# One plain feature block less in three feed-forward openings, and two norm broadcasts moved, in a two-layer encoder kernel

## The chip, the cores and the metric

The kernel runs on one core of one Trainium2 chip. The metric is the device time of one execution in microseconds (us), the median of several. TensorE (PE) does the matmuls, VectorE (DVE), ScalarE (ACT) and GpSimd (POOL) the elementwise work, and SyncE (SP) issues most of the loads of weights from memory.

## What is computed

A bidirectional encoder of two layers, 512 tokens (SEQ) of width 1024 (D_MODEL), all in float32. Each layer has a feed-forward half step, a block of mixers, a second feed-forward half step, and a gated embedding; a norm ends the whole.

```python
def rmsnorm(x, g):
    y = xf * lax.rsqrt(jnp.mean(xf * xf, axis=-1, keepdims=True) + EPS)
    return (y * g.astype(jnp.float32)).astype(x.dtype)
def swiglu(x, w_gate, w_up, w_down):
    return (jax.nn.silu(x @ w_gate) * (x @ w_up)) @ w_down
...
    for i in range(DEPTH):
        h = h + 0.5 * swiglu(rmsnorm(h, ffn1_norm[i]), ffn1_w_gate[i], ffn1_w_up[i], ffn1_w_down[i])
        ...
        h = h + y @ w_out[i]
        h = h + 0.5 * swiglu(rmsnorm(h, ffn2_norm[i]), ffn2_w_gate[i], ffn2_w_up[i], ffn2_w_down[i])
        e = rmsnorm(p[i] @ ple_w_proj[i], ple_post_norm[i])
        gate = jax.nn.sigmoid(rmsnorm(h, ple_gate_norm[i]) @ ple_w_gate[i])
        h = h + gate * e
    return rmsnorm(h, final_norm)
```

The hidden width of the feed-forward is 2816: 22 feature blocks of 128 (NF).

## The kernel before, in words

Activations lie with the features on the 128 partitions and the tokens along the free axis. Every float32 operand is split into a high part (rounded for the matmul, `hi`, names ending in h) and a low part (the rest, `lo`, names ending in l), and a product is three matmuls: high by high, high by low, low by high (`mm3`, L146). ACT makes the high parts (casts), DVE the low parts (L132, `lo_of`).

**Norm.** The sum of squares of a token comes out of a small matmul (`tok`, L195), DVE makes the inverse root (`rtok`, L163), and `bc` (L212) transposes it over all partitions into a bank of PSUM, which ACT copies to `rbc` (L214). The norm is applied after the matmul, since it scales whole tokens.

**A feed-forward** (`ffn`, called four times: ffn1 and ffn2 of layer 0, ffn1 and ffn2 of layer 1) goes through 22 feature blocks. The first `np0` are plain: a block has a gate chunk and an up chunk of weights (`Chunk`: load into `wraw`, cast to `whi` L347, low part `wlo` L132), and each chunk is 24 matmuls of 128x512 (`plain`, L147 to L149). `np0` is PLAIN0 in the first call and PLAIN in the others. A finished plain block is gated (`gated`, L373): DVE multiplies the gate's bank by the norm (L376), ACT takes Silu (L377, with a table load ahead of the first), DVE multiplies by the up bank (L379), ACT makes the high part `ah` (L381) and DVE the low part `al`. `gate(f)` starts this for block f, each `step()` takes every started block one stage on.

The other blocks are made with the Strassen-Winograd scheme: seven products p1 to p7 of half the size in each direction, 12 matmuls of 128x256 each (L597), in place of eight. They need sums of quarters of the weights (`qd` and `qa`, cast and split to `pw`: `parts`, L561 and L132; the sums S2 and S4 by DVE, `sums`, L582 and L584) and sums T1 to T4 of quarters of the input (`quarters` on ACT and POOL, `combined` L397 and L398 on DVE, then high parts `th` L402 and low parts `tl` L132). These input sums are made once per feed-forward, beside the plain blocks: the opening.

The order on TensorE at the first Strassen block u is p1(u), p5(u), p2(u), p6(u), p1(u+1), p7(u), p5(u+1), p4(u), p2(u+1), p3(u), and so on. p5 multiplies T1 with the weights S1. p6 adds into the bank of p1 after ACT copied it to `g1` (L624), and p7 adds into the same bank after ACT copied p6's sum to `g2` (L663). p7's own copy is `c22` (L673).

**What sets the order.** In `ffn` every engine runs its instructions in the order in which the code writes them. Stages are put into a list of items with planned times; loads and weight preparation (`tasks`) are put between the items by their lead times, so ACT and DVE run one fixed row of casts, gating and sums. The openings are `slabs` and `opening(n)` for the first call, `opening2` and `later(n)` for the others (n counts the chunks): in each, the matmuls of chunk n come first, then the next chunks' casts (`beside`), the input sums, `step()` and `gate`.

**The embedding's gate** (`ple`, L1391) for the last layer works on two halves of the tokens, b = 0 and 1, with eight output blocks m each: 24 matmuls of 128x256 per half block. Two norms are needed in its first half: that of h (`st.norm`) and that of the embedding e (`nm`). Banks of PSUM are eight, four each of the kinds `ps` and `pm`; `norm_banks` takes two `pm` banks. `post` multiplies the eight blocks of e by their norm (L1425, DVE), then `gate(i)` finishes a half block (L1417). Here only TensorE follows the written order.

Of the kernel before, what the change touches and what calls it, by code (L numbers as in the profile page):

```python
# [30 lines left out]
HALF = T // 2  # L31
LEAD = 5
H = T // 2
PLAIN = 3
PLAIN0 = 4
GROUPS = (5, 4, 4, 4, 5)
NA = max(GROUPS) + 1
QD = 6
# [28 lines left out]
CH = {}  # L67
# [28 lines left out]
def trunk(ctx: ExitStack, tc, xT, pT, pos, W, gains, cst, dftc, out):  # L96
# [195 lines left out]
            b = slice((base + k) * P, (base + k + 1) * P)  # L292
            mm3(o, hi[:, b], lo[:, b], st.hi[k], st.lo[k], k == 0, k == NK - 1)

    def ffn(l, cgu, cd, st, nxt, first=False):

# [3 lines left out]
        with tc.tile_pool(name="ap", bufs=1) as ap, tc.manual_schedule():  # L302
# [57 lines left out]
                    return [(lead + 6.0, self.load), (lead, prep)]  # L360


            np0 = PLAIN0 if first else PLAIN
            Th, Tl = [], []
            xgs, ts, side = {}, {}, []

            def step():

                for x in list(side):
                    if next(x, None) is None:  # L370
                        side.remove(x)
# [13 lines left out]
            def quarters(i):  # L385
                xg = xgs[i] = tile("pw", 6, [2, T])
                for j in range(2):
                    S.activation(xg[:, j], h[:, i + 4 * j], AF.Copy, scale=st.g(i + 4 * j))
                t = ts[i] = tile("pw", 6, [4, H])
                b11, b12, b22 = xg[:, 0, 0:H], xg[:, 0, H:T], xg[:, 1, H:T]  # L390
                G.tensor_tensor(t[:, 0], b11, b12, op=ALU.subtract)
                G.tensor_tensor(t[:, 1], b22, b12, op=ALU.subtract)

            def combined(i):

                xg, t = xgs.pop(i), ts[i]
                V.scalar_tensor_tensor(t[:, 2], t[:, 0], -1.0, xg[:, 1, H:T], op0=ALU.mult, op1=ALU.subtract)  # L397
                V.scalar_tensor_tensor(t[:, 3], t[:, 2], -1.0, xg[:, 1, 0:H], op0=ALU.mult, op1=ALU.subtract)  # L398

            def combined_high(i):  # L400
                Th.append(tile("th", 4, [4, H], F32R))
                S.copy(Th[i], ts[i])  # L402
# [5 lines left out]
            def gate(f):  # L408
                side.append(gated(f))
                next(side[-1])  # L410

            pairs = []
            chunks = [Chunk(cgu + n) for n in range(2 * np0)]
# [72 lines left out]
            def opening(n):  # L486
                def run():
                    plain(n)
                    beside(n)
                    if n == 4:  # L490
                        combined(3)
                    if n < 6:
                        combined_high(n - 2)
                    step()
                    for f in {5: (0, 1), 6: (2,), 7: (3,)}.get(n, ()):
                        gate(f)
                    if n < 6:
                        combined_low(n - 2)
                    if n == 4:
                        bc()  # L500

                return run

            def opening2():

                for ks in (range(NK - 1), range(NK - 1, NK)):
                    plain(0, ks)
                    plain(1, ks)
                chunks[2].high()
                chunks[2].low()  # L510
                quarters(0)
                quarters(1)
                for i in range(2):
                    combined(i)
                    combined_high(i)
                for i in range(2):
                    combined_low(i)
                tok()
                chunks[3].high()

            def later(n):
                def run():
                    plain(n)
                    beside(n)
                    if n == 2:
                        quarters(2)
                        quarters(3)
                    if n in (2, 3):
                        combined(n)
                        combined_high(n)  # L530
                    step()
                    if n > 2:
                        gate(n - 3)
                    if n in (2, 3):
                        combined_low(n)
                    if n == 2:
                        bc()

                return run
# [75 lines left out]
            def p1(u):  # L615
                U[u] = {"gate": Chunk(cgu + 2 * u)}

                def run():
                    d = U[u]
                    d["B"] = bank("ps")[:, 0:H]  # L620
                    hi, lo = d["gate"].hi, d["gate"].lo
                    product(u, "B", hi[:, 0:T], lo[:, 0:T], "B11", True)
                    d["g1"] = small("g1")
                    S.copy(d["g1"], d["B"])  # L624
                    step()

                return run, U[u]["gate"].tasks(2, 10.1)

            def p5(u):
                def run():  # L630
                    d = U[u]
                    d["E"] = bank("ps")[:, 0:H]
                    p = d["w", "S1"]
                    product(u, "E", p[:, 0], p[:, 1], "T1", True)
                    step()

                def prep():
                    parts(u, "S1")
                    sums(u)

                return run, load(u, "S1", 0, "A22") + [(7.0, prep)]

            def p2(u, after=None):
                def run():
                    d = U[u]
                    d["A"] = bank("pm")[:, 0:H]
                    hi, lo = d["gate"].hi, d["gate"].lo
                    product(u, "A", hi[:, T:2 * T], lo[:, T:2 * T], "B21", True)
                    V.tensor_tensor(d["g1"], d["g1"], d["A"], op=ALU.add)  # L649
                    G.tensor_tensor(d["g1"], d["g1"], st.rb[:, h1], op=ALU.mult)  # L650
                    step()
                    if after is not None:
                        finish2(after)

                return run, []
# [735 lines left out]
    def ple(l, st, nxt):  # L1391


        with tc.tile_pool(name="pp", bufs=2) as pp, tc.manual_schedule(engines={mybir.EngineType.PE}):
# [82 lines left out]
            for b in range(2):  # L1477
                pgs = []
                acc = pp.tile([P, T // 2], F32, tag="acc", name="acc")
                accs.append(acc)  # L1480
                for m in range(NK):
                    if b == 0:
                        raw = pp.tile([P, CHUNK], F32, tag="gr", name="gr", bufs=3)
                        nc.sync.dma_start(raw, W[l, CH["gate"] + m])
                        gw.append((pp.tile([P, CHUNK], F32R, tag="gh", name="gh", bufs=NK),
                                   pp.tile([P, CHUNK], F32R, tag="gl", name="gl", bufs=NK)))
                        split(*gw[m], raw)
                    pgs.append(bank("pm" if m % 2 else "ps")[:, 0:T // 2])
                    for k in range(NK):
                        kb = slice(k * P, (k + 1) * P)  # L1490
                        mm3(pgs[m], gw[m][0][:, kb], gw[m][1][:, kb], st.hi[k][:, half[b]], st.lo[k][:, half[b]],
                            k == 0, k == NK - 1)
                    if b == 0 and m in (0, 2):
                        norm_banks.append(bank("pm"))
                    if b == 0 and m == 0:
                        st.rt = st.norm.tok(pt=norm_banks[0])
                    if b == 0 and m == 2:
                        st.rb = st.norm.bc(st.rt, pb=norm_banks[0])
                        r = nm.tok(pt=norm_banks[1])
                    if b == 0 and m == 3:  # L1500
                        post(r, norm_banks[1])
                    if b == 1 and m == 2:
                        final_tok(0)
                    if b == 1 and m == 4:
                        final_out(0)
                    for i in ((), (), (), (0, 1, 2, 3), (m,))[min(m, 4)] if b == 0 else (m,):
                        gate(i, pgs[i], half[b])
                        sq = acc if i == 0 else pp.tile([P, T // 2], F32, tag="sq", name="sq")
                        S.activation(sq, h[:, i, half[b]], AF.Square)
                        if i < NK - 1:  # L1510
                            S.activation(h[:, i, half[b]], h[:, i, half[b]], AF.Copy, scale=fg(i))
                        if i >= NK - 2:
                            sqs[b].append(sq)
                        elif i:
                            V.tensor_tensor(acc, acc, sq, op=ALU.add)
# [11 lines left out]
    st = stage(0, "ffn1")  # L1527
    for l in range(L):
        s_mix, s_f2, s_pl = stage(l, "mix"), stage(l, "ffn2"), stage(l, "pleg")
        ffn(l, CH["f1gu"], CH["f1d"], st, s_mix, l == 0)  # L1530
        mix(l, s_mix, s_f2)
        ffn(l, CH["f2gu"], CH["f2d"], s_f2, s_pl)
        st = stage(l + 1, "ffn1") if l + 1 < L else None
        ple(l, s_pl, st and st.chunk)
# [135 lines left out]
```

## Time and profile before

| | |
|---|---|
| median of 3 runs | 2003.66 us (2003.05 to 2003.98) |
| the profiled execution | 2003.73 us |
| its span on the core | 2002.0 us |
| mean granted clock of TensorE | 0.996 |
| busy: PE, DVE, ACT, POOL | 1974.2, 1552.8, 1012.5, 412.5 us |
| chain that ended last | PE 92%, DVE 4%, ACT 2% |

The profiled execution lies within the runs; 1.73 us of it are around the span. Times in the views below count from the start of the span. A row of a timeline has the start, the length, the engine, the line, the operation, what it writes and reads, and in brackets the idle time before it with what ended it. An instruction's length overlaps with the next one's start.

### The profile page before, as it was taken

How to read it: one execution, taken by the hardware profiler on the slowest of the kernel's cores; microseconds unless marked ns; L12 is line 12 of the kernel's file. 1: busy time of each engine (PE TensorE's matmuls, PEld its weight loads, DVE VectorE, ACT ScalarE, POOL GpSimd, SP SyncE). 2: the span in 40 equal slices, each digit the busy share in tenths (PEclk: the TensorE clock that was granted, in tenths of full speed). 3: DMA queues.
4: the chain of work that ended last, by engine and by line, in shares of the span. 5: the costliest groups of instructions: out<-in, count | busy, mean ns of one | idle time of the engine just before them, and what ended most of it. 6: DMA issues, size and time to landing. Idle time of an engine off the chain costs nothing.

```text
span 2002.0 us, 32174 instructions
## 1 busy us (share of the span) xinstructions
PE 1974.2 (99%) x12370; PEld 1763.1 (88%) x12370; DVE 1552.8 (78%) x2599; ACT 1012.5 (51%) x1945; POOL 412.5 (21%) x470
## 2 busy tenths in 40 slices
PE   9999999999999999999999999999999999999997
PEld 7999999888789899998888999988977899999987
DVE  7788777677768778877886888776796677778876
ACT  6454445456645344546563444454665554445463
POOL 2132224001002223331021332320000122223400
PEclk9999999999999999999999999999999999999999
DMA  5456653321125555552255556622221266655431
GB/s 188 134 154 158 169 138 103 104 89 42 52 85 153 161 151 149 145 155 95 97 148 142 154 146 152 163 82 93 81 66 47 98 157 158 168 139 153 122 126 43
DMA packets 99707, 248.20 MB, mean 124 GB/s; under 512 B 11184, under 2 KB 14128, under 8 KB 99552
## 3 DMA queue, kind: packets, MB, share of 16 engines
q1 hardware_dynamic: 75216, 203.08, 30.8%
q0 software_dynamic: 21664, 39.56, 12.2%
q10 hardware_dynamic: 2672, 3.49, 0.6%
q8 instruction: 97, 1.59, 0.3%
q14 instruction: 58, 0.48, 0.1%
HBM read 242.42 MB, written 2.10 MB: 122 GB/s over the span
## 4 chain that ended last, share of the span: by engine, by line
PE 92%; DVE 4%; ACT 2%; DMA 1%; issue 1%; ACTq 0%; DVEq 0%; POOL 0%; POOLq 0%; SPq 0%
PE ps L597 32%; PE ps L147 9%; PE ps L148 9%; PE ps L149 9%; PE pm L149 8%; PE pm L147 8%; PE pm L148 8%; PE pm L597 5%; PE ps L827 1%; PE ps L828 1%; PE ps L829 1%; PE ps L1280 1%; DVE wlo L132 1%; DMA wraw<-in_W 1%; PE pm L195 0%
## 5 line engine op out<-in xcount | busy, mean ns | idle before, releaser
L597 PE MATMUL ps<-th,pw 128*128 128x256 f32 x2400 | 457.2, 283 | 1.1 <-ACT c L673 1.1
L132 DVE TENSOR_TENSOR wlo<-wraw,whi 128x1024 fp32r<-128x1024 f32 (+4 forms) x273 | 348.2, 1276 | 53.1 <-ACT whi L347 32.3
L597 PEld LDWEIGHTS ps<-th,pw 128*128 128x128 f32 x2400 | 384.9, 192 | 2.3 <-ACT c L673 1.3
L597 PE MATMUL ps<-tl,pw 128*128 128x256 f32 x1200 | 339.6, 283 | 0.0
L347 ACT CAST whi<-wraw 128x512 fp32r<-128x512 f32 (+1 forms) x260 | 200.5, 802 | 225.6 <-PE pm L148 114.9
L597 PEld LDWEIGHTS ps<-tl,pw 128*128 128x128 f32 x1200 | 229.8, 192 | 1.1
L132 DVE TENSOR_TENSOR pw<-qd,pw 128x512 fp32r<-128x512 f32 x225 | 181.2, 805 | 15.0 <-ACT pw L561 9.7
L573 POOL DMA_DIRECT2D qd<-in_W x150 | 130.9, 927 | 252.0 <-DMA qd<-in_W 242.4
L147 PE MATMUL pm<-ah,whi 128*128 128x512 f32 x392 | 154.7, 395 | 0.0
L149 PE MATMUL pm<-ah,wlo 128*128 128x512 f32 x392 | 154.6, 394 | 0.0
L148 PE MATMUL pm<-al,whi 128*128 128x512 f32 x392 | 154.3, 394 | 0.0
L663 ACT COPY g<-ps 128x256 f32<-128x256 f32 x75 | 27.9, 372 | 224.8 <-PE ps L597 223.4
L135 ACT CAST ah<-g 128x256 fp32r<-128x256 f32 x150 | 59.1, 404 | 151.7 <-DVE g L689 138.9
L561 ACT CAST pw<-qd 128x512 fp32r<-128x512 f32 x225 | 129.6, 616 | 0.0
L135 ACT CAST whi<-wraw 128x1024 fp32r<-128x1024 f32 (+4 forms) x80 | 77.4, 969 | 98.5 <-PE ps L148 48.3
L132 DVE TENSOR_TENSOR pw<-qa,pw 128x512 fp32r<-128x512 f32 x150 | 117.3, 782 | 12.2 <-ACT pw L561 12.2
L147 PE MATMUL ps<-ah,whi 128*128 128x512 f32 x312 | 123.0, 394 | 0.0
L149 PE MATMUL ps<-ah,wlo 128*128 128x512 f32 x312 | 122.9, 394 | 0.0
L148 PE MATMUL ps<-al,whi 128*128 128x512 f32 x312 | 122.8, 394 | 0.0
L597 PE MATMUL ps<-xh,pw 128*128 128x256 f32 x600 | 119.9, 283 | 0.0
L650 POOL TENSOR_TENSOR g<-g,rbc 128x256 f32<-128x256 f32 x75 | 65.8, 878 | 219.3 <-DVE g L649 219.3
L608 POOL TENSOR_TENSOR g<-g,c 128x256 f32<-128x256 f32 x75 | 66.3, 884 | 208.5 <-ACT g L607 208.5
(382 smaller groups left out, 5241.5 us busy)
## 6 DMA issues: line engine op xcount, KB each, us to landing
wraw<-in_W SPq DMA_DIRECT2D x239, 512.0 KB, 3.4
qd<-in_W SPq DMA_DIRECT2D x225, 256.0 KB, 4.2
qd<-in_W POOLq DMA_DIRECT2D x150, 256.0 KB, 4.7
gr<-in_W SPq DMA_DIRECT2D x8, 512.0 KB, 3.7
wraw<-in_W SPq DMA_DIRECT2D x8, 320.0 KB, 3.1
wraw<-in_dftc SPq DMA_DIRECT2D x4, 516.0 KB, 3.3
wraw<-in_W SPq DMA_DIRECT2D x8, 256.0 KB, 3.8
wraw<-in_W SPq DMA_DIRECT2D x4, 408.0 KB, 3.0
```

Source lines behind the costliest of these rows:

```text
L132: V.tensor_tensor(lo, x, hi.bitcast(F32), op=ALU.subtract)
L135: S.copy(hi, x)
L147: mm(o, wh, xh, start=first, stop=False)
L148: mm(o, wh, xl, start=False, stop=False)
L149: mm(o, wl, xh, start=False, stop=last)
L347: S.copy(self.hi[:, b], self.raw[:, b])
L561: S.copy(p[:, 0], U[u][src])
L573: nc.gpsimd.dma_start(U[u][name], up[:, T:2 * T] if add == "A22" else gate[:, 0:T], accum_op=ALU.add)
L597: mm(U[u][o], x[:, b], y, start=first and i + j == 0, stop=i == 3 and j == 2, skip_group_check=not first)
L608: G.tensor_tensor(d["g2"], d["g2"], d["c22"], op=ALU.mult)
L650: G.tensor_tensor(d["g1"], d["g1"], st.rb[:, h1], op=ALU.mult)
L663: S.copy(d["g2"], d["B"])
```

## The change

PLAIN goes from 3 to 2 and PLAIN0 from 4 to 3 (three of the four feed-forwards have one plain block less and one Strassen block more); the third call, ffn1 of layer 1 (`late`), keeps three, and there the norm's broadcast and the input sums are spread over one chunk more. The gated blocks' stages are put by a table, `plan`, of which the places S1, S2 and S3 are behind p1, p5 and p2 of the first Strassen block; `None` is a `step()`, a number a `gate`. In `ple` of the last layer the broadcast of h's norm and the sums of e's norm come behind half block 3 and not 2, `post` and the first gates behind half block 5 and not 3, and the first half's final norm two half blocks later in the second half. Lines behind L412 move by 7 to 10: the product's matmul is L604, the casts L568, the copies of `g1`, `g2` and `c` L631, L673 and L683, the sums L589 and L591.

```diff
-PLAIN = 3
-PLAIN0 = 4
+PLAIN = 2
+PLAIN0 = 3
...
-    def ffn(l, cgu, cd, st, nxt, first=False):
+    def ffn(l, cgu, cd, st, nxt, first=False, late=False):
...
-            np0 = PLAIN0 if first else PLAIN
+            np0 = PLAIN0 if first or late else PLAIN
...
+            S1, S2, S3 = 100, 101, 102
+            plan = ({5: (0, 1), S1: (None, None, 2), S2: (None,), S3: (None,)} if first else
+                    {4: (0, 1), 5: (None, None, 2), S1: (None,), S2: (None,)} if late else
+                    {3: (None, 0), S1: (None, 1), S2: (None,), S3: (None,)})
+
+            def gating(n):
+
+                for f in plan.get(n, ()):
+                    step() if f is None else gate(f)
...
                     if n < 6:
                         combined_high(n - 2)
-                    step()
-                    for f in {5: (0, 1), 6: (2,), 7: (3,)}.get(n, ()):
-                        gate(f)
+                    gating(n)
...
-                for i in range(2):
+                for i in range(2 - late):
                     combined(i)
                     combined_high(i)
...
                     if n == 2:
                         quarters(2)
+                    if n == 2 + late:
                         quarters(3)
-                    if n in (2, 3):
-                        combined(n)
-                        combined_high(n)
-                    step()
-                    if n > 2:
-                        gate(n - 3)
-                    if n in (2, 3):
-                        combined_low(n)
-                    if n == 2:
+                    if n - late in (1, 2, 3)[not late:]:
+                        combined(n - late)
+                        combined_high(n - late)
+                    gating(n)
+                    if n - late in (1, 2, 3)[not late:]:
+                        combined_low(n - late)
+                    if n == 2 + late:
                         bc()
...
                     S.copy(d["g1"], d["B"])
-                    step()
+                    if u == np0:
+                        gating(S1)
...
-                    if b == 0 and m in (0, 2):
+                    if b == 0 and m in (0, 3):
                         norm_banks.append(bank("pm"))
...
-                    if b == 0 and m == 2:
+                    if b == 0 and m == 3:
                         st.rb = st.norm.bc(st.rt, pb=norm_banks[0])
                         r = nm.tok(pt=norm_banks[1])
-                    if b == 0 and m == 3:
+                    if b == 0 and m == 5:
                         post(r, norm_banks[1])
-                    if b == 1 and m == 2:
+                    if b == 1 and m == 4:
                         final_tok(0)
-                    if b == 1 and m == 4:
+                    if b == 1 and m == 6:
                         final_out(0)
-                    for i in ((), (), (), (0, 1, 2, 3), (m,))[min(m, 4)] if b == 0 else (m,):
+                    for i in (range(6) if m == 5 else range(max(6, m), m + 1)) if b == 0 else (m,):
...
-        ffn(l, CH["f1gu"], CH["f1d"], st, s_mix, l == 0)
+        ffn(l, CH["f1gu"], CH["f1d"], st, s_mix, l == 0, l > 0)
```

ACT in the opening of ffn2, layer 0, before: from the second stage of the first gated block (its table load and Silu stand just ahead) to the copy of `g2`, which is the last row (`qa` holds the gated block; `pw<-qd` is the cast of a loaded weight sum, the first one p5's).

```order
L381 CAST ah<-qa 128x512
L377 ACTIVATE qa<-qa 128x512
L347 CAST whi<-wraw 128x512 x2
L381 CAST ah<-qa 128x512
L377 ACTIVATE qa<-qa 128x512
L561 CAST pw<-qd 128x512
L347 CAST whi<-wraw 128x512 x2
L561 CAST pw<-qa 128x512
L624 COPY g_6645<-ps 128x256
L381 CAST ah<-qa 128x512
L561 CAST pw<-qd 128x512 x3
L663 COPY g_6712<-ps 128x256
```

The same place now, from the table load to the copy of `g2`:

```order
L377 ACT_TABLE_LOAD
L377 ACTIVATE qa<-qa 128x512
L568 CAST pw<-qd 128x512
L347 CAST whi<-wraw 128x512 x2
L568 CAST pw<-qa 128x512
L631 COPY g_6640<-ps 128x256
L381 CAST ah<-qa 128x512
L377 ACTIVATE qa<-qa 128x512
L568 CAST pw<-qd 128x512
L381 CAST ah<-qa 128x512
L568 CAST pw<-qd 128x512 x2
L673 COPY g_6714<-ps 128x256
```

The cast for p5 moved from behind three Silu and two `ah` to behind the first Silu, and one gated block (Silu and `ah`) is gone; the second block's stages stand between the first Strassen casts.

DVE at the same place, before, from the first gated block's L376 on:

```order
L376 TENSOR_TENSOR qa<-ps,rbc 128x512
L132 TENSOR_TENSOR tl<-pw,th 128x1024
L132 TENSOR_TENSOR wlo<-wraw,whi 128x1024
L379 TENSOR_TENSOR qa<-pm,qa 128x512
L376 TENSOR_TENSOR qa<-ps,rbc 128x512
L132 TENSOR_TENSOR wlo<-wraw,whi 128x1024
L132 TENSOR_TENSOR al<-qa,ah 128x512
L379 TENSOR_TENSOR qa<-pm,qa 128x512
L376 TENSOR_TENSOR qa<-ps,rbc 128x512
L132 TENSOR_TENSOR pw<-qd,pw 128x512
L582 TENSOR_TENSOR qa<-wraw,qd 128x512
L584 TENSOR_TENSOR qa<-wraw,qa 128x512
```

And now:

```order
L376 TENSOR_TENSOR qa<-ps,rbc 128x512
L132 TENSOR_TENSOR tl<-pw,th 128x1024
L132 TENSOR_TENSOR pw<-qd,pw 128x512
L589 TENSOR_TENSOR qa<-wraw,qd 128x512
L591 TENSOR_TENSOR qa<-wraw,qa 128x512
L132 TENSOR_TENSOR wlo<-wraw,whi 128x1024
L132 TENSOR_TENSOR pw<-qa,pw 128x512
L379 TENSOR_TENSOR qa<-pm,qa 128x512
L376 TENSOR_TENSOR qa<-ps,rbc 128x512
L132 TENSOR_TENSOR pw<-qd,pw 128x512
L132 TENSOR_TENSOR al<-qa,ah 128x512
L379 TENSOR_TENSOR qa<-pm,qa 128x512
```

The low part for p5 (`pw<-qd,pw`) and the sums now come ahead of the first L379; the second L376 stands behind p6's low part, and the second L379 behind p7's.

TensorE in the last layer's `ple`, before: the end of half block 2, the broadcast (L212), the sums of squares (L195), the start of half block 3.

```order
L149 MATMUL ps<-xh,gl 128x256
L212 MATMUL pm<-cs,rtok 128x128 x4
L195 MATMUL pm<-ones,sqacc 128x1 x4
L147 MATMUL pm<-xh,gh 128x256
L148 MATMUL pm<-xl,gh 128x256
```

And now, where the half block ahead of the broadcast is the third (`pm`) and the one behind it the fourth (`ps`):

```order
L149 MATMUL pm<-xh,gl 128x256
L212 MATMUL pm<-cs,rtok 128x128 x4
L195 MATMUL pm<-ones,sqacc 128x1 x4
L147 MATMUL ps<-xh,gh 128x256
L148 MATMUL ps<-xl,gh 128x256
```

The broadcast and the sums moved past one half block of 24 matmuls.

## Rows read from the trace of the kernel before

**Rows 1.** Busy time, share of the span and instructions of each engine, from the page.

```profile
PE 1974.2 (99%) x12370; PEld 1763.1 (88%) x12370; DVE 1552.8 (78%) x2599; ACT 1012.5 (51%) x1945; POOL 412.5 (21%) x470
```

**Rows 2.** Waits of TensorE: us in total, times, longest us.

```profile
PE pm L212 <- DVE rtok L163: 3.6, 2, 2.6
...
PE ps L597 <- ACT c L673: 1.1, 1, 1.1
```

**Rows 3.** TensorE's timeline and chain of waits (start, us, what), ffn2 of layer 0.

```profile
612.86 0.39 PE L147 MATMUL ps<-xh,whi 128*128 128x512 f32 x1
...
618.43 0.39 PE L147 MATMUL pm<-xh,whi 128*128 128x512 f32 x1
...
637.09 8.60 PE ps L597 x72
...
647.10 8.62 PE ps L597 x72
```

**Rows 4.** ACT's timeline in the opening of ffn2, layer 0.

```profile
607.78 1.05 ACT L402 CAST th<-pw 128x1024 fp32r<-128x1024 f32 x1 [3.70 <-DVE pw L398]
608.73 0.59 ACT L214 ACTIVATE rbc<-pm 128x512 f32<-128x512 f32 x1
...
612.10 1.05 ACT L402 CAST th<-pw 128x1024 fp32r<-128x1024 f32 x1 [0.19 <-DVE pw L398]
613.17 1.28 ACT L377 ACT_TABLE_LOAD   x1
614.46 0.63 ACT L377 ACTIVATE qa<-qa 128x512 f32<-128x512 f32 x1
...
622.07 0.60 ACT L561 CAST pw<-qd 128x512 fp32r<-128x512 f32 x1
...
628.23 1.66 ACT L561 CAST pw<-qd 128x512 fp32r<-128x512 f32 x3
629.93 0.37 ACT L663 COPY g<-ps 128x256 f32<-128x256 f32 x1
```

**Rows 5.** DVE's timeline in the same opening.

```profile
610.00 1.22 DVE L132 TENSOR_TENSOR wlo<-wraw,whi 128x1024 fp32r<-128x1024 f32 x1
...
611.59 0.42 DVE L398 SCALAR_TENSOR_TENSOR pw<-pw 128x256 f32<-128x256 f32 x1
611.93 0.69 DVE L376 TENSOR_TENSOR qa<-ps,rbc 128x512 f32<-128x512 f32 x1
613.18 1.22 DVE L132 TENSOR_TENSOR tl<-pw,th 128x1024 fp32r<-128x1024 f32 x1 [0.57 <-ACT th L402]
...
622.71 0.69 DVE L132 TENSOR_TENSOR pw<-qd,pw 128x512 fp32r<-128x512 f32 x1 [1.21 <-ACT pw L561]
623.32 0.69 DVE L582 TENSOR_TENSOR qa<-wraw,qd 128x512 f32<-128x512 f32 x1
...
626.99 0.68 DVE L379 TENSOR_TENSOR qa<-pm,qa 128x512 f32<-128x512 f32 x1
```

**Rows 6.** Timelines of TensorE and ACT, opening of ffn1, layer 0.

```profile
38.48 0.60 PE L212 MATMUL pm<-cs,rtok 128*128 128x128 f32 x4
...
39.77 1.05 ACT L347 CAST whi<-wraw 128x1024 fp32r<-128x1024 f32 x1
```

**Rows 7.** Tail and an earlier gap: timeline, windows (busy, clock, DMA), chain.

```profile
1945.96 0.65 PE L212 MATMUL pm<-cs,rtok 128*128 128x128 f32 x4 [2.57 <-DVE rtok L163]
...
1948.00:1951.00 3.00, 3.00 (x16) 3.00 (x16) 1.95 (x12) 1.27 (x3) 0.00 (x0) 0.50 0.00 0
...
1947.40 0.23 PE pm L147
...
1951.88 0.44 PE pm L212 x4
...
515.67 0.33 PE L1280 MATMUL ps<-cs,prob 128*128 128x128 f32 x1 [1.91 <-DVE prob L1272]
...
516.00:520.00 4.00, 4.00 (x23) 3.32 (x23) 3.86 (x7) 2.66 (x7) 0.00 (x0) 1.00 0.36 131
```

More of the change, by code (lines that the diff above doesn't have):

```diff
@@ L512, in opening2 @@
                 quarters(1)
-                for i in range(2):
+                for i in range(2 - late):
                     combined(i)
                     combined_high(i)
-                for i in range(2):
+                for i in range(2 - late):
                     combined_low(i)
@@ L634, in run @@
                     product(u, "E", p[:, 0], p[:, 1], "T1", True)
-                    step()
+                    if u == np0:
+                        gating(S2)
                 def prep():
@@ L650, in run @@
                     G.tensor_tensor(d["g1"], d["g1"], st.rb[:, h1], op=ALU.mult)
-                    step()
+                    if u == np0:
+                        gating(S3)
                     if after is not None:
```

## The prediction

> **What bounds the kernel now.** I read four views of the profile, from coarse to fine. The busy shares first [rows 1]: TensorE is busy for 99% of the span, VectorE (DVE) for 78%, ScalarE (ACT) for 51%. So nearly every microsecond of TensorE work that goes is won, and what DVE and ACT do is free as long as TensorE doesn't wait for it. The waits next [rows 2]: TensorE waits for a norm's `rtok` twice, 3.6 us in all, the longest 2.6, and once for 1.1 us behind the copy of `c`. Those are what the change can win by moving work. The chain of waits and TensorE's timeline give the pace: a plain chunk runs from 612.86 to 618.43, 5.57 us, so a plain block of two takes 11.14; seven Strassen products of 12 matmuls run from 637.09 to 647.10, 10.01 us, or 1.43 for one [rows 3]. Last, the timelines of ACT and DVE in an opening [rows 4, 5]: the reader is to see that the two queues are not slack there. They make the input sums' splits, the gated blocks and the first Strassen weights one after another, each handing on to the other, and the last of this, the copy at 629.93, ends at 630.3, 1 us ahead of the p7 that needs it (five products on from a p1 at about 624.1: 631.3). The share of 51% says nothing about this stage.
>
> **The blocks.** Three openings lose a plain block and gain a Strassen block: 3 x (11.14 - 10.01) = 3.4 us less TensorE work.
>
> **The three shortened openings.** The work of ACT and DVE shrinks by one gated block, but TensorE arrives at the first Strassen products 11.14 us earlier. I replay the new order with the durations of the rows; an instruction that follows another without a wait costs about 0.08 less than its length, as the rows' starts show.
>
> Opening of ffn2, layer 0, on the clock of the profile. The plain chunk at 612.86 is gone, so p1 is due there, p5 at 614.30, p7 (five products on) at 620.04 [rows 3].
> - ACT: `th` 607.78, `rbc` from 608.73, then the chunk's cast in halves to 610.4 (it was one cast, and later). DVE: `tl` to 610.0, `wlo` when the cast is there, 610.4 to 611.6, the last two sums of 0.42 to 612.4. ACT's last `th` starts there, 612.5 to 613.6; it waited for DVE before, too [rows 4, 5]. The table load of 1.28 ends at 614.9, the first Silu at 615.4, and only then comes the cast of p5's weights: 616.0, with DVE's low part at 616.75. The third matmul of p5, due at 614.5, reads it: **2.3 us of waiting**. In the run before, the same cast stood at 622.07, ahead of a p5 at 625.4.
> - From there DVE has in its row: both sums of 0.69, a `wlo` (1.22), p6's low part, the up-product L379, L376 of the second gated block, to 621.0 (p6 waits 0.15). ACT: its Silu to 621.6, p7's weight cast to 622.2. DVE: low part, `al`, L379 to 624.1. ACT: `ah`, two casts, and then the copy of `g2`, from 625.76 to 626.13. p7 adds into the bank that this copy empties, so it starts at 626.2 and not at 620.04. **Together 6.15 us.**
> - Lower bound: were DVE never to wait, its work from 611.6 to that L379 is 9.4 us (2 x 0.45, L376 and L379 2 x 0.61 each, `tl` 1.15, three low parts and `al` 4 x 0.61, the sums 1.32, `wlo` 1.14), which ends at 621.0; `ah`, two casts and the copy follow, 2.0 us: p7 at 623.0, 3.0 us late. Upper bound: the 6.15 and what the clock adds below. I take 6.15, since every hand-over in it is in the order and has its length from a row.
>
> The opening of ffn2, layer 1, has the same order: 6.15 again. In ffn1 of layer 0, `bc` is at 38.48 and the chunk's cast at 39.77 [rows 6]; p1 is due a chunk after the broadcast, at 44.5, p7 at 51.7. Two gated blocks are made in the last chunk here, so p5 is met with 0.6 to spare, but DVE does two L379, two `al`, L376, a low part and another L379 before the `ah`, casts and copy: p7 starts at 56.4, **4.7 us late** (2.6 if DVE never waited).
>
> The Trainium skill, "ScalarE: Activation LUTs", section "What ACT_TABLE_LOAD costs", puts a drain of about 1.4 us behind each table load of 1.28. The trace agrees on the load and not on the drain: Silu starts 0.01 us after it [rows 4]. By the page p5 would wait 1.4 longer in both ffn2 openings, an estimate of 2.8 us more; the row speaks against it, so it has no share of the chances.
>
> **The late opening** (ffn1, layer 1). It keeps three plain blocks. The norm's broadcast, which waited about 1 us for `rtok` [rows 2], stands a chunk later and doesn't wait; with the slowed matmuls behind it some 1.4 us are won. The price: gated blocks 0 and 1 are now both started behind the fifth chunk, and the casts for p5 stand behind them, so by the same replay p5 to p7 wait 3.2 us in all. The 1.1 us wait behind the copy of `c` [rows 2] then falls inside this. Sum: -1.4 + 3.2 - 1.1 = +0.7; bounds -2.1 (no new wait) and +2.7 (the wait behind `c` goes on as well, and some).
>
> **The tail.** TensorE stands still for 2.57 us ahead of 1945.96, and then the granted clock is 0.50 from 1948 to 1951, the 1.2 GHz level: the half block from 1947.40 to 1951.88 takes 4.48 us, where 24 matmuls of this shape take 24 x 8.60/72 = 2.87 [rows 3, 7]. With the broadcast one half block later, TensorE comes to it at 1943.4 + 2.87 = 1946.3, after `rtok` (1945.9): both go, 2.57 + 1.6 = **4.2 us won**. What is late next: the gates start behind `post`, whose rescaling now follows m = 5 instead of 3. They come about 1.5 us later while TensorE is 4.2 earlier; of the eight banks two are the norm's, six hold half blocks, and the seventh waits for the first gate. I find no wait there, since a gate takes DVE three instructions on half a block, against 2.87 of TensorE. The second half's norm is moved along with its squares.
>
> **The clock in the openings.** Behind the 2.57 us gap the clock fell and cost 1.6 us; behind a gap of 1.91 (ahead of 515.67) it was 1.00 from 516 to 520 [rows 7]. The gaps expected here before p7 are 3.75, 3.75 and 4.7 us: longer than the one that cost 1.6. I take 1.5 for each of three, **+4.5**; bounds 0 and 1.6 each. The Trainium skill, "TensorE: Matmul & The Clock Gate", section "Why this matters for your kernels", speaks against any change that opens such gaps: idle stretches between bursts of matmuls bring the clock to its lower level. The trace agrees at the one gap and not at the shorter one.
>
> **Sum** against the profiled execution (2003.73 us, of which 2002.0 are span; the median of the runs is 2003.66, so 0.07 less): -3.4 (blocks) + 4.7 + 2 x 6.15 (waits before p5 and p7) + 0.7 (late opening) - 4.2 (tail) + 4.5 (clock) = +14.6: **2018.3 us**, 0.7% slower.
>
> **Rivals.**
> - *The waits are there, the clock stays up.* 2018.3 - 4.5 = 2013.8; with the lower bounds of the waits (2.6 + 2 x 3.0) 2005.5. For it: the waits come in two pieces with work between, and the 1.91 gap cost nothing.
> - *The queues keep up (faster).* If nothing waits before p5 and p7, what is left is -3.4, the late opening's -2.1 and the tail's -4.2: 1994.0; with the late opening at 0.7, 1996.8. It decides where all three openings together wait less than 2.9 us (to win 4 us). For it: DVE is busy 78% and ACT 51% [rows 1], and the copy of `g2` was just in time before. Against: the table load, the Silu and the cast stand in one row behind a `th` that can't come sooner, and 9.4 us of DVE work doesn't fit.
> - *The tail gives its gain back.* The gates wait for `post`, TensorE for a bank. If the 4.2 us are lost there: 2022.5. Against: six banks of cover.
> - *The parts cancel.* Half of the waits and no clock: 2003.7 - 3.4 + 8.5 + 0.7 - 4.2 = 2005.3, near no change.
>
> **How the numbers follow.** The forecast has 0.55 (2015 to 2021), the waits without the clock or near their lower bounds 0.22 (2006 to 2014), the tail's loss 0.06, the cancelling 0.07, the faster rival 0.10. About 0.2% (4 us) is what a measurement of this kernel can tell from no change: faster 0.10, same 0.08 (the cancelling, and a part of the second case's low end), slower 0.82. The range reaches from the low end of the second case to the tail's loss, 2006 to 2023, and leaves the faster rival and most of the cancelling out.
>
> **What would show it.** In the waits of TensorE: a new wait of L604 (the product) for `pw`'s low part, 1.5 to 2.5 us, twice, and one for the copy of `g2` (ACT L673), 3 to 5 us, three times, each with DVE's L379 and ACT's `ah` right before; a granted clock near 0.50 after them; no 2.6 us wait of L212 and no 0.50 at 1948. It would be wrong if L604's waits come to less than 7 us in all, if the waits are there but p7 is released by something else, or if TensorE waits in the tail for a gate.

## The result, and the profile after

The changed kernel takes 2018.59 us (median of 5 runs, 2016.14 to 2019.53) against 2003.88 for the kernel before (median of 5 runs): ratio 1.0072, 95% interval [1.0059, 1.0086]. It is slower, by about 14.5 us. The profiled execution has a span of 2016.5 us against 2002.0, and a mean granted clock of 0.993.

The busy row of the page, to be read beside [rows 1]:

```profile
PE 1979.6 (98%) x12478; PEld 1772.3 (88%) x12478; DVE 1566.3 (78%) x2626; ACT 1019.5 (51%) x1975; POOL 424.6 (21%) x485
```

TensorE has 108 instructions more (three times 84 matmuls in place of 48), as the exchange of blocks says; the shares of ACT and DVE are as before. The loss can't be seen here. It stands in TensorE's waits (us in total, times, longest), beside [rows 2]:

```profile
PE ps L604 <- ACT g L673: 8.5, 3, 4.4
...
PE ps L604 <- ACT pw L568: 3.0, 2, 1.5
...
PE ps L604 <- issue: 1.9, 1, 1.9
PE ps L604 <- DVE pw L132: 0.7, 3, 0.2
```

The wait of L212 for `rtok` is gone, and so is the one behind the copy of `c`. New are 8.5 us behind the copy of `g2` (three times), 3.0 us for `pw` (twice), and one of 1.9 us. TensorE's timeline has them: p7 in ffn1 of layer 0, p5 and p7 in ffn2 of layer 0, p5 in ffn1 of layer 1, p7 in ffn2 of layer 1:

```profile
55.24 0.58 PE L604 MATMUL ps<-th,pw 128*128 128x256 f32 x1 [4.38 <-ACT g L673]
...
619.97 0.39 PE L604 MATMUL ps<-th,pw 128*128 128x256 f32 x1 [1.50 <-ACT pw L568]
...
620.70 0.50 PE L604 MATMUL ps<-th,pw 128*128 128x256 f32 x2 [0.22 <-DVE pw L132]
...
630.01 0.39 PE L604 MATMUL ps<-th,pw 128*128 128x256 f32 x1 [2.07 <-ACT g L673]
...
1042.50 0.60 ACT L568 CAST pw<-qd 128x512 fp32r<-128x512 f32 x1
1043.20 0.36 PE L604 MATMUL ps<-th,pw 128*128 128x256 f32 x1 [1.85 <-issue]
...
1624.18 0.38 PE L604 MATMUL ps<-th,pw 128*128 128x256 f32 x1 [2.06 <-ACT g L673]
```

The one at 1043.20, put down to "issue", starts as ACT's cast of p5's weights (1042.50, 0.60 long) is done. ACT in the opening of ffn2, layer 0, beside [rows 4]; the broadcast stands at 610.88 now (606.84 before):

```profile
616.41 1.05 ACT L402 CAST th<-pw 128x1024 fp32r<-128x1024 f32 x1 [2.14 <-DVE pw L398]
617.48 1.28 ACT L377 ACT_TABLE_LOAD   x1
618.78 0.63 ACT L377 ACTIVATE qa<-qa 128x512 f32<-128x512 f32 x1
619.32 0.60 ACT L568 CAST pw<-qd 128x512 fp32r<-128x512 f32 x1
...
624.34 0.62 ACT L381 CAST ah<-qa 128x512 fp32r<-128x512 f32 x1 [2.12 <-DVE qa L379]
...
625.48 0.60 ACT L568 CAST pw<-qd 128x512 fp32r<-128x512 f32 x1
...
628.04 0.62 ACT L381 CAST ah<-qa 128x512 fp32r<-128x512 f32 x1 [1.96 <-DVE qa L379]
628.56 1.13 ACT L568 CAST pw<-qd 128x512 fp32r<-128x512 f32 x2
629.60 0.36 ACT L673 COPY g<-ps 128x256 f32<-128x256 f32 x1
```

The reader sees the chain: `th`, table load, Silu, the cast for p5 ending at 619.92, where p5 starts at 619.97; then two `ah`, each held up by about 2 us for DVE's L379, casts, and the copy of `g2` ending at 629.96, where p7 starts at 630.01.

The granted clock behind these waits (each row: the window, its length, the busy time of PE, PEld, which is TensorE's weight load, DVE, ACT and POOL with the number of instructions, then the granted clock as a share of full speed, DMA share, GB/s):

```profile
55.00:58.00 3.00, 2.76 (x13) 2.76 (x14) 2.96 (x6) 2.02 (x5) 1.06 (x2) 0.50 0.40 117
...
620.00:624.00 4.00, 3.78 (x21) 3.57 (x22) 3.96 (x6) 1.85 (x4) 0.62 (x1) 0.70 0.82 133
...
630.00:632.00 2.00, 1.99 (x16) 1.99 (x17) 1.97 (x4) 2.00 (x5) 0.29 (x1) 1.00 0.19 39
...
1616.00:1618.00 2.00, 2.00 (x11) 2.00 (x10) 2.00 (x4) 0.39 (x2) 0.00 (x0) 0.50 0.76 147
...
1626.00:1628.00 2.00, 2.00 (x11) 2.00 (x11) 2.00 (x3) 1.30 (x3) 1.74 (x2) 0.50 0.93 304
...
1964.00:1967.00 3.00, 3.00 (x28) 2.95 (x27) 1.33 (x8) 1.56 (x2) 0.00 (x0) 1.00 0.00 0
```

It is at 0.50, the lower level of 1.2 GHz, behind p7's wait in the first opening, below 1 behind p5's in both ffn2 openings, at 0.50 behind p7's in the fourth feed-forward (ffn2 of layer 1) and not in the second (ffn2 of layer 0). In the tail, where it was 0.50 [rows 7], it is 1.00 now.

Both spans cut at the same instructions (the norm's broadcast of each feed-forward, the next norm's sums of squares):

| stretch | before, us | after, us | difference |
|---|---|---|---|
| start to the first broadcast | 38.48 | 37.51 | -1.0 |
| ffn1, layer 0, from the broadcast | 332.63 | 337.52 | +4.9 |
| mixers, layer 0 | 235.73 | 235.85 | +0.1 |
| ffn2, layer 0, from the broadcast | 347.36 | 352.53 | +5.2 |
| embedding, layer 0 | 52.76 | 52.76 | 0.0 |
| ffn1, layer 1 | 351.05 | 352.21 | +1.2 |
| mixers, layer 1 | 235.00 | 236.68 | +1.7 |
| ffn2, layer 1, from the broadcast | 343.58 | 350.15 | +6.6 |
| last embedding to the end | 65.41 | 61.29 | -4.1 |

The differences add up to the 14.5 us of the spans. Each column is one profiled execution.

### The profile page after: what moved, and what is told of

It reads as the page before. It is cut to its first block, busy times and chain, and to the rows that moved or that the text cites. A ratio compares the mean times of both kernels' runs of the same rounds, so it can differ in the third digit from the quotient of the medians.

```text
span 2016.5 us, 32493 instructions
## 1 busy us (share of the span) xinstructions
PE 1979.6 (98%) x12478; PEld 1772.3 (88%) x12478; DVE 1566.3 (78%) x2626; ACT 1019.5 (51%) x1975; POOL 424.6 (21%) x485
## 4 chain that ended last, share of the span: by engine, by line
PE 89%; DVE 5%; ACT 3%; issue 1%; DMA 1%; ACTq 0%; DVEq 0%; POOL 0%; POOLq 0%
PE ps L604 33%; PE ps L147 8%; PE ps L148 8%; PE ps L149 8%; PE pm L149 7%; PE pm L147 7%; PE pm L148 7%; PE pm L604 5%; DVE wlo L132 1%; PE ps L837 1%; PE ps L838 1%; PE ps L839 1%; PE ps L1290 1%; PE pm L195 0%; PE pm L1125 0%
## 5 line engine op out<-in xcount | busy, mean ns | idle before, releaser
L604 PE MATMUL ps<-th,pw 128*128 128x256 f32 x2496 | 480.9, 285 | 14.1 <-ACT g L673 8.5
L604 PEld LDWEIGHTS ps<-th,pw 128*128 128x128 f32 x2496 | 403.8, 193 | 17.1 <-ACT g L673 9.1
L604 PE MATMUL ps<-tl,pw 128*128 128x256 f32 x1248 | 354.9, 284 | 0.0
L604 PEld LDWEIGHTS ps<-tl,pw 128*128 128x128 f32 x1248 | 241.1, 193 | 1.1
L132 DVE TENSOR_TENSOR pw<-qd,pw 128x512 fp32r<-128x512 f32 x234 | 190.4, 814 | 18.0 <-ACT pw L568 12.5
L580 POOL DMA_DIRECT2D qd<-in_W x156 | 136.5, 931 | 220.0 <-DMA qd<-in_W 218.0
L673 ACT COPY g<-ps 128x256 f32<-128x256 f32 x78 | 29.0, 372 | 225.4 <-PE ps L604 223.5
L568 ACT CAST pw<-qd 128x512 fp32r<-128x512 f32 x234 | 135.0, 616 | 0.0
L132 DVE TENSOR_TENSOR pw<-qa,pw 128x512 fp32r<-128x512 f32 x156 | 122.9, 788 | 11.7 <-ACT pw L568 11.5
L604 PE MATMUL ps<-xh,pw 128*128 128x256 f32 x624 | 124.6, 283 | 0.0
```

The costliest lines, as they stand in the source:

```text
L132: V.tensor_tensor(lo, x, hi.bitcast(F32), op=ALU.subtract)
L568: S.copy(p[:, 0], U[u][src])
L580: nc.gpsimd.dma_start(U[u][name], up[:, T:2 * T] if add == "A22" else gate[:, 0:T], accum_op=ALU.add)
L604: mm(U[u][o], x[:, b], y, start=first and i + j == 0, stop=i == 3 and j == 2, skip_group_check=not first)
L673: S.copy(d["g2"], d["B"])
```

## The experiments

The theory: three openings ask ACT and DVE for Strassen operands before their fixed rows of instructions get to them, the start of p7 is set by the copy of `g2`, and the clock falls behind some of these waits; the tail is a true gain. The rivals: the tail gains nothing; each wait is a cost of its own; ACT and DVE have too much to do as a whole, whatever their order; the clock plays no part.

**The tail alone** (the changed part of `ple` in the kernel before):

```diff
...
-                    if b == 0 and m == 2:
+                    if b == 0 and m == 3:
                         st.rb = st.norm.bc(st.rt, pb=norm_banks[0])
                         r = nm.tok(pt=norm_banks[1])
-                    if b == 0 and m == 3:
+                    if b == 0 and m == 5:
                         post(r, norm_banks[1])
...
```

> The kernel before with the last embedding's part of the change alone. Theory (the 2.57 us wait for rtok and the clock that fell behind it both go, and the later gates cost nothing): 4.2 us less than before, about 1999.6, no L212 wait of 2.6 us and no clock of 0.50 behind half block 3. Rival (post and the gates come too late and hand the gain back): within 1 us of before, with a new wait of TensorE in the last 60 us.

Measured: 1998.93 us against 2004.38, ratio 0.9972 [0.9961, 0.9984]: 5.5 us less by the medians, 3.2 to 7.8 by the interval, which holds the 4.2. TensorE's broadcast and the clock behind it:

```profile
1944.86 0.65 PE L212 MATMUL pm<-cs,rtok 128*128 128x128 f32 x4
...
1944.00:1947.00 3.00, 3.00 (x27) 2.85 (x26) 1.33 (x8) 1.44 (x2) 0.00 (x0) 1.00 0.02 5
1947.00:1950.00 3.00, 3.00 (x27) 3.00 (x27) 1.85 (x11) 1.17 (x3) 0.00 (x0) 1.00 0.00 0
```

No wait stands in the row of L212, and the clock stays at 1.00. In the profile the stretch from the last embedding to the end takes 61.27 us against 65.41, 4.1 less. What the medians show beyond that need not be the tail's: in this profile ffn1 of layer 1, whose code is the same as before, is 1.3 us shorter too (of which more at the next experiment). The tail is a gain, and this version is the fastest of all: 0.3% better than the kernel before.

**The third opening alone** (the `late` part in the kernel before):

```diff
...
+            plan = ({4: (0, 1), 5: (None, None, 2), S1: (None,), S2: (None,)})
...
-        ffn(l, CH["f1gu"], CH["f1d"], st, s_mix, l == 0)
+        ffn(l, CH["f1gu"], CH["f1d"], st, s_mix, l == 0, l > 0)
```

> The kernel before with the third opening's part of the change alone (broadcast, input sums and gated blocks of ffn1, layer 1, spread over a chunk more). Theory (the wait for rtok and the wait behind the copy of c go, but p5's cast comes late behind two gated blocks started together, and the clock falls behind that): 1 us more than before, 0 to 2, with a wait of 1.5 to 2.5 us ahead of p5. Rival (the two waits that go are a gain): 2 us less than before.

Measured: 2005.34 us against 2004.27, ratio 1.0004 [0.9995, 1.0013]. The runs can't tell it from no change; the gain of 2 us is excluded. In the profile the stretch of ffn1, layer 1, is 352.15 us against 351.05, 1.1 more, and a wait ahead of p5 stands in place of the two others:

```profile
PE ps L609 <- issue: 2.0, 1, 2.0
...
1036.00:1038.00 2.00, 2.00 (x11) 2.00 (x11) 1.97 (x4) 0.89 (x2) 0.00 (x0) 0.50 0.94 141
```

1.99 us of waiting and a clock of 0.50 behind it eat what the broadcast gained. The 1.1 us wait behind the copy of `c`, which the part was to take away, is not a fixed cost. In the profile of before ACT was late for that copy because a load of weights landed late:

```profile
1041.12 1.14 ACT L347 CAST whi<-wraw 128x512 fp32r<-128x512 f32 x2 [2.12 <-DMA wraw<-in_W]
```

In the profile of the tail alone, where this opening's code is unchanged, ACT doesn't wait there, the wait behind the copy of `c` is absent, and the stretch takes 349.71 us. Against that execution the third opening's part costs 2.4 us, and not 1.1.

**p5's cast earlier** (the changed kernel, the two ffn2 openings):

```diff
-                return run, load(u, "S1", 0, "A22") + [(7.0, prep)]
+                early = u == np0 and not first and not late
+                return run, load(u, "S1", 0, "A22") + ([(7.1, lambda: parts(u, "S1")), (7.0, lambda: sums(u))] if early
+                                                       else [(7.0, prep)])
```

> The changed kernel with the cast of p5's weights ahead of the last th, the table load and the first Silu, in the two ffn2 openings alone. Theory (the start of p7 is set by the copy of g2, which stands behind the second gated block's ah on ACT, so that the wait ahead of p5 is only taken out of the wait ahead of p7): the waits of p5 go, p7 starts about 0.9 us earlier against the broadcast, its wait grows from 2.1 to about 5 us; 0 to 2 us less than the changed kernel, 2016.5 to 2018.5. Rival (each wait is a cost of its own, with its fall of the clock): 7 us less, about 2011.5.

Measured: 2018.68 us, ratio 1.0069 [1.0055, 1.0083] to the kernel before, against 1.0072 of the changed kernel: no gain that could be told. The cast is at 613.86 now, and:

```profile
613.86 0.62 ACT L568 CAST pw<-qd 128x512 fp32r<-128x512 f32 x1
...
621.57 0.39 PE L604 MATMUL ps<-th,pw 128*128 128x256 f32 x1 [0.57 <-ACT g L631]
...
628.91 0.58 PE L604 MATMUL ps<-th,pw 128*128 128x256 f32 x1 [3.38 <-ACT g L675]
...
630.00:632.00 2.00, 2.00 (x12) 2.00 (x12) 2.00 (x4) 0.81 (x3) 1.40 (x2) 0.56 0.69 207
```

p5's wait is gone; p6 waits 0.57 and again 0.57, and p7 3.38 in place of 2.07. Against the broadcast (610.57 here) p7 starts 18.34 us later, in the changed kernel 19.13: 0.8 earlier, where 0.9 was expected. (p7's wait was expected at 5 us; p6's waits took a part of it.) The wait ahead of p5 was indeed no cost of its own: the copy of `g2` (L675 here) sets when p7 starts. Nor is all of the 0.8 won: the clock now falls behind p7's longer wait in this opening (0.56 over 630 to 632, where the changed kernel had 1.00), and the stretch of ffn2 takes 352.76 us in layer 0, 0.2 more than in the changed kernel, and 349.23 in layer 1, 0.9 less.

**The copy first** (the changed kernel, three openings: the last gated block's L379, `ah` and `al` behind the copy of `g2`):

```diff
...
                     S.copy(d["g2"], d["B"])
+                    if u == np0 and not late:
+                        step()
...
```

> The changed kernel with the last gated block's up-product, ah and al put behind the copy of g2 in three openings, nothing else. Theory (p7 waits for that copy because ACT stands behind ah, which waits for DVE's L379): the waits ahead of p7 go from 2.1, 2.1 and 4.4 us to 0, 0 and about 2.4; 6 us less, and up to 3 more where the clock no longer falls: 2009.5 to 2012.5. Rival (DVE's work as a whole is too much for the time, so that p7 or the next product waits for another of its results): less than 2 us gained, with new waits of L604 for pw or c.

Measured: 2019.68 us, ratio 1.0073 [1.006, 1.0086]. The theory's 6 us are not there. The waits:

```profile
PE ps L604 <- ACT c L685: 8.2, 3, 2.9
...
PE ps L604 <- ACT g L673: 2.6, 2, 2.4
...
52.85 0.39 PE L604 MATMUL ps<-th,pw 128*128 128x256 f32 x1 [2.40 <-ACT g L673]
...
58.48 0.58 PE L604 MATMUL ps<-th,pw 128*128 128x256 f32 x1 [2.49 <-ACT c L685]
```

p7's waits behave as expected (2.40 in the first opening, none in the ffn2 openings). But p4, which adds into the same bank once ACT has copied `c` out of it, now waits 2.5 to 2.9 us in each of the three. ACT in the first opening says why:

```profile
52.44 0.36 ACT L673 COPY g<-ps 128x256 f32<-128x256 f32 x1
55.71 0.62 ACT L381 CAST ah<-qa 128x512 fp32r<-128x512 f32 x1 [2.91 <-DVE qa L379]
...
58.06 0.37 ACT L685 COPY c<-ps 128x256 f32<-128x256 f32 x1
```

The same `ah` waits 2.91 us for DVE, and now the copy of `c` stands behind it. Two readings were left: there is too much work, or the `ah` must go behind this copy as well.

**The steps later still** (behind the copy of `c`, `al` behind p4):

```diff
...
                     S.copy(d["c22"], d["B"])
+                    if u == np0 and not late:
+                        step()
...
                     product(u, "B", p[:, 0], p[:, 1], "T4", False)
+                    if u == np0 and not late:
+                        step()
```

> The changed kernel with the last gated block's up-product and ah behind the copy of c (not only of g2), and its al behind p4, in three openings. Theory (what matters is what stands ahead of the two copies on ACT): no wait or under 0.5 us for either copy in the ffn2 openings, about 2.4 ahead of p7 in the first opening; 5 to 8 us less than the changed kernel, 2010.5 to 2013.5. Rival (ACT and DVE have too much to do as a whole between the broadcast and the second Strassen block, and the wait moves on with whatever is put last): under 2 us less, with a wait of 1.5 us or more at another product.

Measured: 2013.3 us, ratio 1.0046 [1.0032, 1.0059]: 5.3 us less than the changed kernel by the medians, inside what the theory said; the two were timed beside different runs of the kernel before, and their intervals just touch, at 1.0059. In the profile the three shortened openings together are 4.1 us shorter than in the changed kernel.

```profile
53.28 0.39 PE L604 MATMUL ps<-th,pw 128*128 128x256 f32 x1 [2.39 <-ACT g L673]
...
625.49 0.39 PE L604 MATMUL ps<-th,pw 128*128 128x256 f32 x1 [0.80 <-ACT g L673]
...
PE ps L604 <- DVE g L714: 1.8, 2, 0.9
```

p7 waits 2.39 in the first opening, as expected, and not at all in ffn2 of layer 1; in ffn2 of layer 0 it waits 0.80, where under 0.5 was expected. p4 doesn't wait. Two blocks on, a product waits 0.9 for a bank that DVE's sum into `g2` (L714 here) still has to empty, twice: a piece of the wait does move on, as the rival had it, but it is the smaller piece.

**Both** (the steps later and p5's cast earlier):

> The same with the cast of p5's weights ahead of the last th and the table load too, in the two ffn2 openings. Theory: the waits ahead of p5 go as well, p7 waits about 1 us in the ffn2 openings: 7 to 11 us less than the changed kernel, 2007.5 to 2011.5, still slower than the kernel before without its tail. Rival (too much to do as a whole): as much as with the later steps alone, since the wait ahead of p5 comes back ahead of p7 or p4.

Measured: 2011.11 us, ratio 1.0039 [1.0027, 1.0052]; its intervals overlap with those of the steps alone, so the 2 us between the two are not shown by the runs. The profiles have the two ffn2 stretches 0.8 us shorter each than with the steps alone. With p5's wait gone, p6 waits 1.1 and p7 0.80:

```profile
626.28 0.39 PE L604 MATMUL ps<-th,pw 128*128 128x256 f32 x1 [0.80 <-ACT g L675]
...
640.02 0.39 PE L604 MATMUL ps<-th,pw 128*128 128x256 f32 x1 [0.86 <-DVE g L716]
```

By the stretches of the table the three shortened openings cost 3.2, 3.8 and 3.9 us in this version, 11.0 together, and 16.6 in the changed kernel: the order was about a third of the loss in them. In what remains no wait is longer than 2.4 us, and they sit at other hand-overs, which is what the rival said. That too much work is the reason for all of it is not shown: no order tried here makes a shorter opening pay, but not every order was tried.

**Filler** (matmuls nobody reads while TensorE waits; they write the other half of p5's bank and start a new sum there, so the first Strassen block of three feed-forwards computes something else, and this version serves for its times alone):

```diff
+            def filler(u, n):
+                for i in range(4 * n):
+                    mm(U[u]["E2"][:, H:T], U[u]["gate"].hi[:, 0:P], st.hi[0][:, 0:H], start=True, stop=True)
...
+                    if u == np0 and not first and not late:
+                        filler(u, 3)
...
+                    if u == np0 and not late:
+                        filler(u, 6)
```

> The changed kernel with matmuls whose result nobody reads, in an unused half of p5's bank: 12 ahead of the first p5 in the two ffn2 openings, 24 ahead of the first p7 in three openings, in the time in which TensorE waits. Theory (part of the loss is the clock that falls behind these waits): p7 still starts with the copy of g2, but the clock stays at 1.00 behind it: 1 to 4 us less than the changed kernel, 2014.5 to 2017.5. Rival (the clock plays no part): 0, or some us more for the added matmuls.

Measured: 2017.32 us, ratio 1.0062 [1.005, 1.0075], 1.3 us less than the changed kernel by the medians; the interval overlaps with the changed kernel's, so the runs alone don't decide. The profile does. Its clock column reads 0.95 over the whole feed-forwards, at the pace that reads 1.00 in the changed kernel (36 matmuls in the 4 us from 200 to 204 in both), and it doesn't fall behind these waits:

```profile
55.00:58.00 3.00, 2.88 (x24) 2.88 (x25) 2.97 (x6) 2.32 (x7) 1.18 (x2) 0.95 0.35 112
...
620.00:624.00 4.00, 3.72 (x29) 3.31 (x28) 3.38 (x5) 2.48 (x6) 0.45 (x1) 0.95 0.91 131
...
1626.00:1628.00 2.00, 2.00 (x17) 1.82 (x17) 2.00 (x2) 0.93 (x2) 1.37 (x2) 0.95 0.87 273
...
55.12 0.39 PE L604 MATMUL ps<-th,pw 128*128 128x256 f32 x1 [1.61 <-ACT g L680]
...
1623.81 0.39 PE L604 MATMUL ps<-th,pw 128*128 128x256 f32 x1 [0.60 <-ACT g L680]
```

p7 still starts with the copy of `g2` (L680 here), 17.74 us behind the broadcast in the first opening and 19.14 in ffn2 of layer 1; in the changed kernel it is 17.73 and 19.12. So what this version wins, it wins behind p7.

The stretches: ffn1 of layer 0 takes 336.37 us and ffn2 of layer 1 takes 348.99, both 1.2 less than in the changed kernel, and ffn2 of layer 0 takes 352.70, 0.2 more. The gain stands in the two openings where the clock had been at 0.50 behind p7, and not in the one where it had not.

## Why the prediction was right

The time (2018.3 forecast, 2018.59 measured) and the mechanism came out, and two of the sizes did not: the clock's term, and the sum of wait and clock in one opening. The waits of the product (L604) come to 14.1 us in all, against the 7 below which the prediction called itself wrong. The parts, one by one:

- **Blocks, -3.4.** The instruction counts bear out the exchange. At a clock of 1.00 the pace of a Strassen product is as before, so this term was not in question.
- **First opening.** p7's wait was forecast at 4.7 us and is 4.38. With the block's 1.1 less and 1.5 for the clock this gave +5.1; the stretch shows +4.9.
- **The ffn2 openings.** p7 was forecast 19.36 us behind the broadcast (606.84 to 626.2) and comes 19.13 and 19.12 behind it. The wait ahead of p5 is 1.5 and another 0.2, where 2.3 was counted up to the third matmul. (The Silu starts at 618.78 right behind the table load, 617.48 and 1.28 long. The drain that the Trainium skill puts there, in "ScalarE: Activation LUTs", section "What ACT_TABLE_LOAD costs", is not seen in this trace either.) But the wait ahead of p7 is 2.07 in layer 0 and 2.06 in layer 1, and not 3.75, nor in the range of 3 to 5 named as a sign: in both the clock fell already behind p5's wait (0.70 over 620 to 624, 0.50 over 1616 to 1618), TensorE came later to p7, and a part of the wait was filled with slow work. So the step that counted "6.15 of waiting" and "1.5 of clock" as two terms was mis-sized in the second opening: +6.5 forecast, +5.2 measured, since the clock was back at 1.00 from 630 on. In the fourth it fell a second time behind p7 and the stretch shows +6.6.
- **The clock, +4.5.** Filler shows that it is a cost of its own: 1.2 us came back in each of two openings and nothing in the third, 2.3 in place of 4.5. The term counted three falls of 1.5 us; two of them cost anything, 1.2 us each. The stretches leave room for a little more: p7's delay explains +3.5, +4.8 and +5.0 of the three openings (its distance from the broadcast, with one Strassen block of 10.05 added, against 24.30, 24.34 and 24.18 before), and 1.4, 0.3 and 1.6 are left, 3.3 in all. What the 1.0 between the two is, no run shows.
- **Late opening, +0.7.** +1.2 in the changed kernel, +1.1 alone. The wait ahead of p5 is 1.9 and 0.2 in place of 3.2 in all, and the clock, not counted there, makes up for it. The term of -1.1 for the wait behind the copy of `c` rested on one execution: with the tail alone that wait is absent from the same code, and measured from there the part costs 2.4. That this term came out is in part luck.
- **Tail, -4.2.** -4.1, and shown alone. The gates came later and nothing waited for them.
- **Not in the sum:** -1.0 at the start, where the wait for the first weights differs from run to run (1.44 us before, 0.28 here, 1.39 with the third opening alone), and +1.7 in the mixers of layer 1, of which below. They nearly cancel, as did the errors of the parts; the match to 0.3 us is better than the parts deserve.

The faster rival fell: the queues don't keep up, though their mean shares are 78% and 51%. The rival in the tail fell. The rival whose clock stays up fell by what the filler gave back, though in one opening of three the clock indeed cost nothing.

## What to carry to other kernels

Shortening a prologue takes away the time in which other engines get ready; replay their queues, in order, with measured lengths, before counting the matmuls saved. An in-order engine that has to empty a bank should do that ahead of work that waits for another engine, and moving the waiting work back only helps once it is behind every such copy: behind one alone, the wait turned up in front of the next product no smaller than it had been (2.85 us in place of 2.07 in ffn2 of layer 0). Parts of a change should be timed alone: here one part gains 0.3%, and the others together lose about 1%.

## What was not expected of the hardware

The same wait may or may not bring the clock down. In both kernels TensorE stands still for 1.91 or 1.92 us in the attention of each layer. In the changed kernel the clock stayed up behind it in layer 0 and fell in layer 1; the last row is the same place of layer 1 in the profile of before:

```profile
520.00:522.00 2.00, 2.00 (x11) 1.59 (x11) 1.97 (x5) 1.10 (x2) 0.00 (x0) 1.00 0.79 258
...
1512.00:1514.00 2.00, 1.60 (x5) 1.31 (x6) 1.97 (x7) 1.19 (x2) 0.00 (x0) 0.62 0.48 158
1514.00:1516.00 2.00, 2.00 (x7) 1.49 (x6) 1.26 (x2) 0.00 (x0) 0.00 (x0) 0.53 0.28 109
...
1502.00:1504.00 2.00, 2.00 (x10) 1.59 (x11) 1.97 (x6) 1.20 (x2) 0.00 (x0) 1.00 0.78 258
```

That is the better part of the +1.7 us of those mixers, which the change doesn't touch; in the profile of before neither of the two fell. It is a matter of the execution: in the profiles of the third opening alone, of both and of the filler the clock fell in layer 0, and there the mixers of layer 0 take 1.3, 1.4 and 2.0 us more than before. So a difference of 1 to 2 us between two single profiles can be this, and not the change. Ahead of p5, too, waits of 1.5 and 0.2 us were followed by a lower clock in the changed kernel (0.70 over 620 to 624) and not with the steps later:

```profile
620.00:624.00 4.00, 4.00 (x34) 3.84 (x33) 2.95 (x5) 1.88 (x5) 0.00 (x0) 1.00 0.83 209
```

So the length of a gap alone doesn't tell its cost in clock. What else decides was not tried. The advice of the Trainium skill, "TensorE: Matmul & The Clock Gate", section "Why this matters for your kernels", to leave no idle stretches between bursts of matmuls, is borne out by what the filler gave back (2.3 us).
